# TensorE in source order, the other engines left to the build's scheduler: a two-layer FoX and NSA trunk

## The chip, the cores and the metric

The kernel runs on one core of one Trainium2 chip. A core has five engines that run at the same time, each with an instruction queue of its own: TensorE (PE; its weight loads are listed apart as PEld), VectorE (DVE), ScalarE (ACT), GpSimd (POOL) and SyncE (SP), which here issues nearly all DMAs. An engine works through its queue in order and waits at an instruction whose inputs have not been signalled. The metric is device time in microseconds (us) of one execution.

## The reference

The input is x, 512 tokens of 1024 channels. Each of two layers computes, all causal and in float32:

```
h    = rmsnorm(x);  proj = h @ w_in        # q,k,v,f | q_b, 6 x kv | gates
FoX:   8 heads of 64; s = q.k/8 + c_i - c_j, c = cumsum(log_sigmoid(f + b)); softmax; @ v
NSA:   8 query heads, 2 key heads, rope:
       compressed: blocks of 32 tokens -> gelu MLP -> one key/value a block; softmax over 31 blocks
       selected:   top min(16, 8) of 8 blocks of 64, so all causal keys
       window:     512 tokens, so all causal keys
       o = g0*o_c + g1*o_s + g2*o_w
mixed = sigmoid(ga) * (o_fox @ w_o_fox) + sigmoid(gb) * (o_nsa @ w_o_nsa)
x   += mixed @ w_out
x   += relu(rmsnorm(x) @ w_up)**2 @ w_down # 1024 -> 4096 -> 1024
```

A last rmsnorm follows the second layer. With 512 tokens the selection keeps every block and the window reaches every earlier token, so both branches are causal attention over 512 keys with their own keys and values.

## The kernel before

Activations lie transposed: channels on the 128 partitions, the 512 tokens along the free dimension. Nearly every product is split: a float32 operand becomes a rounded high part and a low part, and h·h, h·l and l·h are summed in PSUM. `gemm` (L212 to L214) does this for one output block of 128 channels: 8 blocks of the inner dimension times three products of 128x512, 24 in all; it is a generator that yields after every 6 products. Weights come by DMA in pieces of 128x1024 (`fetch`, L170), ACT rounds the high part (L186) and DVE subtracts the low part (L187) one piece ahead of its use.

PSUM has eight banks, handed out under four names with two buffers each: mm, S, PT, O. SBUF tiles are handed out by tag with a fixed number of buffers; the tag hl (a rounded key or query pair) has one, the tag e (scores of one head) two.

The source emits the work of a layer in this order.

1. `token_proj` multiplies for the FoX values (L315 to L317, 8 steps of 12 products of 128x512). `rstd` turns the sums of squares into the rmsnorm factor: column sums on PE (L267), a short chain on DVE and ACT (L270 to L278), and a broadcast on PE (L283). In layer 0 `rstd` is called after all 8 steps of the projection, in layer 1 after 6, with the other two emitted inside it, between L267 and L283. A second `token_proj` (128x288) gives the NSA values, forget logits and gates.
2. `forget` computes log_sigmoid of 32 columns in some 16 small DVE operations (L644 to L655), the running sum over tokens as products with a triangle (L662) and with ones (L661), and splits it into the tile CC (L663, L664).
3. `fox_proj(0)` projects the key pair and the query pair of the first two FoX heads. `k_pair` scales the projection (L336), rounds it into hl (L342, L343), copies it to the tile kd by four DMAs (L353) and adds two rows of CC (L357). `q_pair` does the same with four copies to q (L366) and two to qx (L375).
4. `attend` runs the eight FoX heads in rounds. Unit t (a head) gives its scores, four steps of two products (L392, L395), followed on DVE and ACT by mask and maximum (L398), exponential (L399) and, after the fourth, reciprocal and scaling (L403, L408). In the same rounds unit t-1 gives its transposes on PE (L421, three steps, read by L430 and L431), and unit t-2 its value products (L447, four steps). A unit takes five rounds. After each round the fill is advanced by 1.8 steps on average (`FOX_FILL`): further projections (`fox_proj(1)` to `(3)`, kc, vc, ks, two query pairs, kw), and, alternating with them, the steps of `compress`: block products with the compression weights (L525) and at its end, with no yield in between, transposes (L532), a gelu on DVE and ACT (L534 to L548), and two small products (L554, L558). Before a unit's first score the fill is advanced until the unit's projections have been emitted. What is left of the fill is emitted at the end.
5. A second `attend` runs 16 NSA units (a selected and a window branch for each head) with 0.95 fill steps a round (`NSA_FILL`). Its fill begins with `cmp_probs(0)`: scores against the compressed keys (L586), a copy (L589), transposes (L593), a softmax over blocks (L596 to L608) and transposes back (L612), all in one step. It goes on with gate projections (L838 scales them) and halves of the FoX output projection, the last two query pairs, `cmp_probs(1)` and eight more gate projections. A window branch ends with two products for the compressed values (L815).
6. The NSA output projection, the mix, and `wout`.
7. `mlp`: 8 plain blocks of `w_up` with `rstd` after the second, 12 blocks of the down projection, then 12 units in Strassen's form (L1196, seven products of 12 each) with the remaining down projections between the products, then the rest of `w_down`. The second layer ends in `last`, which does the final rmsnorm in two halves of 256 tokens.

This order is only the order of emission. `TileContext` records the instructions and their dependencies, and when the context closes the build's scheduler sets the order of every engine's queue: it plays the program through a model of the chip and gives each engine, among the instructions that are ready in the model, the one emitted earliest. So an engine's queue may have an instruction ahead of one that the source emits earlier. All of this happens in the build; on the chip the queues are fixed.

In the printed source, `go` starts with ten products on a tile of ones (L1087) before any data has arrived. The lines that the change touches stand in `build`:

Of the kernel before, what the change touches and what calls it, by code (L numbers as in the profile page):

```python
# [1284 lines left out]
def build(arrays):  # L1285
    nc = bacc.Bacc("TRN2", target_bir_lowering=False, num_devices=1)
    a = {k: nc.dram_tensor(k, v.shape, mybir.dt.from_np(v.dtype), kind="ExternalInput").ap()
         for k, v in arrays.items()}
    a["yT"] = nc.dram_tensor("yT", (2, 128, KT, T // 2), F32, kind="ExternalOutput").ap()
    with tile.TileContext(nc) as tc, ExitStack() as ctx:  # L1290
        Body(ctx, tc, nc, a).go()
    return nc


# [6 lines left out]
```

## Time and profile before

| what | value |
| --- | --- |
| median of 3 runs | 1554.0 us (1553.79 to 1554.16) |
| profiled execution | 1552.95 us |
| its span, first to last instruction | 1551.2 us |
| PE busy | 1536.4 us, 99% |
| PEld busy | 1306.6 us, 84% |
| DVE busy | 1075.2 us, 69% |
| ACT busy | 776.0 us, 50% |
| POOL busy | 205.2 us, 13% |
| mean granted TensorE clock | 0.998 |
| read from HBM | 140.77 MB |

The page gives the busy time of each engine and, in 40 slices, how busy each was. Its chain of waits goes back from the last instruction and is 95% PE. Matmuls are pipelined: a product of 128x512 is listed with some 0.39 us and the next begins some 0.23 us after it, so lengths overlap, and spacing is read from the start times. In the rows of the timeline the first number is the start, the second the length; out<-in are the program's names of tiles, and a bracket at the end gives the idle time of the engine before the row and what ended it. The rows of the view by stretches give the stretch, its length, the busy time of PE, PEld, DVE, ACT and POOL with the number of instructions, the granted clock, the DMA share and GB/s. The rows of the waits name who waited for whom, with total, number of times and longest.

### The profile page before, as it was taken

What the parts mean: (1) busy time and instruction counts of PE and PEld (TensorE: products, weight loads), DVE (VectorE), ACT (ScalarE), POOL (GpSimd) and SP (SyncE); (2) the same over time, 40 slices, a digit from 0 to 9 for tenths busy, and PEclk for the clock granted to TensorE, in tenths of its full rate; (3) what the DMA queues carried; (4) which work ended last, traced back from release to release, by engine and by line L of the source; (5) the groups of instructions that cost most, each with busy time, mean ns of one, the idle gap of its engine ahead of it and who ended that gap; (6) DMA issues with size and microseconds to landing.
All of it is one profiled execution on the core that took longest, in us unless ns stands there. A gap on an engine that the chain in (4) does not pass through costs nothing.

```text
span 1551.2 us, 22739 instructions
## 1 busy us (share of the span) xinstructions
PE 1536.4 (99%) x8460; PEld 1306.6 (84%) x8460; DVE 1075.2 (69%) x2204; ACT 776.0 (50%) x1455; POOL 205.2 (13%) x177
## 2 busy tenths in 40 slices
PE   9999999999999999999999999999999999999997
PEld 8877888888888999999887688888888889999997
DVE  5687988766569776664646789887664887766643
ACT  6444655553454555444433456555434635545553
POOL 4000000000201232221400000000002013222222
PEclk9999999999999999999999999999999999999999
DMA  7545422133333322321535543221433333323131
GB/s 240 172 128 154 127 82 82 55 114 117 96 95 123 109 96 95 109 82 64 176 117 165 157 140 100 68 82 55 150 95 95 95 120 99 113 91 99 65 96 55
DMA packets 56638, 169.57 MB, mean 109 GB/s; under 512 B 7344, under 2 KB 8112, under 8 KB 56528
## 3 DMA queue, kind: packets, MB, share of 16 engines
q1 hardware_dynamic: 53072, 161.84, 33.5%
q10 hardware_dynamic: 3456, 6.29, 1.2%
q8 instruction: 66, 1.08, 0.3%
q14 instruction: 44, 0.36, 0.1%
HBM read 140.77 MB, written 4.19 MB: 93 GB/s over the span
## 4 chain that ended last, share of the span: by engine, by line
PE 95%; DVE 3%; ACT 1%; issue 1%; POOL 0%; DMA 0%; DVEq 0%; SPq 0%; POOLq 0%; ACTq 0%
PE ps_mm L212 12%; PE ps_mm L213 12%; PE ps_mm L214 12%; PE ps_S L1196 4%; PE ps_O L1196 4%; PE ps_O L447 4%; PE ps_mm L1196 3%; PE ps_PT L421 3%; PE ps_PT L1196 3%; PE ps_S L212 3%; PE ps_S L213 3%; PE ps_S L214 3%; PE ps_PT L212 3%; PE ps_PT L213 3%; PE ps_PT L214 3%; PE ps_O L212 3%
## 5 line engine op out<-in xcount | busy, mean ns | idle before, releaser
L186 ACT CAST wh<-raw 128x1024 fp32r<-128x1024 f32 (+2 forms) x187 | 192.6, 1030 | 263.7 <-issue 58.5
L187 DVE TENSOR_TENSOR wl<-raw,wh 128x1024 fp32r<-128x1024 f32 (+2 forms) x187 | 226.6, 1212 | 49.8 <-ACT wh L186 48.9
L212 PE MATMUL ps_mm<-uh,wh 128*128 128x512 f32 x512 | 205.1, 401 | 0.0
L214 PE MATMUL ps_mm<-uh,wl 128*128 128x512 f32 x512 | 202.3, 395 | 0.0
L213 PE MATMUL ps_mm<-ul,wh 128*128 128x512 f32 x512 | 202.1, 395 | 0.0
L399 ACT ACTIVATE E<-E,mx 128x128 f32<-128x128 f32 x192 | 108.0, 563 | 82.7 <-DVE mx L398 75.6
L430 ACT CAST pth<-ps_PT 128x512 fp32r<-128x512 f32 x144 | 73.0, 512 | 94.7 <-PE ps_PT L421 94.4
L212 PEld LDWEIGHTS ps_mm<-uh,wh 128*128 128x128 f32 x512 | 96.2, 188 | 26.5 <-issue 10.6
L214 PEld LDWEIGHTS ps_mm<-uh,wl 128*128 128x128 f32 x512 | 96.2, 188 | 20.4 <-issue 0.8
L213 PE MATMUL ps_mm<-ol,wh 128*128 128x512 f32 (+1 forms) x288 | 111.5, 387 | 1.5 <-POOL ol L1263 1.5
L212 PE MATMUL ps_mm<-oh,wh 128*128 128x512 f32 (+1 forms) x288 | 111.8, 388 | 0.0
L214 PE MATMUL ps_mm<-oh,wl 128*128 128x512 f32 (+1 forms) x288 | 111.2, 386 | 0.0
L398 DVE CUSTOM_DVE_ANT_0 E<-ps_S,ct 128x128 f32<-128x128 f32 x192 | 92.2, 483 | 26.5 <-PE ps_S L395 25.0
L213 PEld LDWEIGHTS ps_mm<-ul,wh 128*128 128x128 f32 x512 | 96.4, 188 | 15.1
L431 DVE TENSOR_TENSOR ptl<-ps_PT,pth 128x512 fp32r<-128x512 f32 x144 | 85.0, 595 | 27.6 <-ACT pth L430 27.2
L1187 DVE TENSOR_TENSOR sl<-s,sh 128x512 fp32r<-128x512 f32 x96 | 76.6, 801 | 36.6 <-ACT sh L1186 36.3
L1263 POOL TENSOR_TENSOR ol<-c,oh 128x512 fp32r<-128x512 f32 x48 | 62.7, 1306 | 295.9 <-ACT oh L1262 268.3
L1186 ACT CAST sh<-raw 128x512 fp32r<-128x512 f32 x72 | 44.7, 620 | 106.3 <-PE ps_S L1196 48.1
L1186 ACT CAST sh<-s 128x512 fp32r<-128x512 f32 x96 | 59.3, 620 | 56.4 <-PE ps_PT L1196 19.3
L253 POOL TENSOR_TENSOR acc<-sq 128x512 f32<-128x512 f32 (+1 forms) x6 | 8.4, 1394 | 595.0 <-DVE wl L187 580.1
L421 PE MATMUL ps_PT<-ct,E 128*128 128x128 f32 x480 | 82.9, 273 | 1.4 <-DVE ptl L431 1.4
L421 PEld LDWEIGHTS ps_PT<-ct,E 128*128 128x128 f32 x480 | 60.1, 140 | 14.8 <-DVE ptl L431 4.2
(441 smaller groups left out, 4068.0 us busy)
## 6 DMA issues: line engine op xcount, KB each, us to landing
raw<-wb SPq DMA_DIRECT2D x64, 512.0 KB, 3.2
raw<-wup SPq DMA_DIRECT2D x64, 512.0 KB, 3.7
raw<-wd SPq DMA_DIRECT2D x48, 512.0 KB, 3.5
kd<-hl SPq DMA_DIRECT2D x48, 256.0 KB, 4.6
w<-w SPq DMA_DIRECT2D x32, 256.0 KB, 5.8
q<-hl SPq DMA_DIRECT2D x64, 128.0 KB, 3.2
raw<-wo SPq DMA_DIRECT2D x16, 512.0 KB
raw<-wout SPq DMA_DIRECT2D x16, 512.0 KB, 3.6
```

The source lines that it names most:

```text
L186: nc.scalar.copy(h[:, :n], raw[:, :n])
L187: nc.vector.tensor_tensor(lo[:, :n], raw[:, :n], h[:, :n].bitcast(F32), op=OP.subtract)
L212: mm(ps, h[:, c], xh, start=start and i == 0, stop=False)
L213: mm(ps, h[:, c], xl, start=False, stop=False)
L214: mm(ps, lo[:, c], xh, start=False, stop=stop and i == ks - 1)
L398: nc.vector.tensor_tensor_reduce(e, ps[:, :n], self.mask[:, T - n:], -1.0, BIG, OP.add, OP.min, mx)
L399: nc.scalar.activation(e, e, AF.Exp, bias=mx, scale=-1.0, accum_out=sm[:, i:i + 1])
L421: nc.tensor.transpose(ps[:, j * 128:(j + 1) * 128], E[i][:, b * 128:(b + 1) * 128], self.ident)
L431: nc.vector.tensor_sub(lo[:, o:o + n], ps[:, :n], h[:, o:o + n].bitcast(F32))
L1186: nc.scalar.copy(h, src)
L1187: nc.vector.tensor_tensor(lo, src, h.bitcast(F32), op=OP.subtract)
L1196: self.nc.tensor.matmul(ps, w, x, skip_group_check=True, **kw)
```

## The change

The body is traced inside a manual-schedule block for one engine. Instructions of TensorE that are emitted inside it keep the order of emission in TensorE's queue. The orders of DVE, ACT, POOL and SP are still chosen by the build's scheduler, which plays the same program with TensorE's order given. No instruction, shape, tile or buffer count is changed.

```diff
     with tile.TileContext(nc) as tc, ExitStack() as ctx:
-        Body(ctx, tc, nc, a).go()
+        with tc.manual_schedule(engines={mybir.EngineType.PE}):
+            Body(ctx, tc, nc, a).go()
     return nc
```

## The prediction

> **What bounds the kernel now.** I read the page's busy table and slices first, then what TensorE (PE) waits for, the stretches at both ends of the run, and then the timeline at each place where the source puts a dependent product right behind what it depends on.
>
> ```profile
> span 1551.2 us, 22739 instructions
> PE 1536.4 (99%) x8460; PEld 1306.6 (84%) x8460; DVE 1075.2 (69%) x2204; ACT 776.0 (50%) x1455; POOL 205.2 (13%) x177
> ...
> PE   9999999999999999999999999999999999999997
> ```
>
> PE is the bound, and it is busy in every slice: 14.8 us of the span are idle.
>
> ```profile
> 0.00:5.80 5.80, 4.64 (x20) 4.34 (x20) 1.40 (x4) 3.23 (x5) 4.82 (x13) 1.00 0.64 186
> 1536.00:1545.20 9.20, 6.59 (x54) 6.26 (x52) 1.95 (x8) 2.83 (x8) 1.48 (x2) 1.00 0.00 0
> 1545.20:1551.20 6.00, 0.00 (x0) 0.00 (x0) 2.43 (x8) 0.00 (x0) 0.00 (x0) 0.50 0.49 175
> ```
>
> The stretches by time (first figures: length, then PE busy) put 1.2 + 2.6 + 6.0 = 9.8 us of that idle time at the two ends. Only 5.0 us lie in the 1530 us between. Each chain of small vector work in there is covered by products that stand later in the source.
>
> ```profile
> PE ps_O L525 <- DVE ca L511: 1.4, 2, 0.7
> PE ps_O L283 <- DVE rcol L278: 1.4, 1, 1.4
> ```
>
> These two rows of the waits show what a waiting product does: PE stood 1.4 us at L283 in all, with the rest of that projection's products behind it. A product that waits holds what is queued after it. [...]
>
> **The change, part by part.** No instruction is added or removed; only PE's order changes. So the cost is the sum of chains that lose their cover, and the gain is at most the 5.0 us above. I take each chain from the trace, subtract vector work that stands in it only because products ran meanwhile, and subtract what the source itself emits in between. The two layers have the same code and the rows are of the first, so each term counts twice.
>
> *Forget gate.* The source calls `forget` (L662, L661) before the first key and query projections. PE runs 39 of those later products first:
>
> ```profile
> 42.64 0.30 PE L317 MATMUL ps_O<-wh,ul 128*128 128x288 f32 x1
> 42.77 0.39 PE L212 MATMUL ps_PT<-uh,wh 128*128 128x512 f32 x1
> 51.41 0.39 PE L214 MATMUL ps_PT<-uh,wl 128*128 128x512 f32 x1
> 51.88 0.38 PE L662 MATMUL ps_S<-ct,f 128*8 128x128 f32 x2
> ```
>
> ```profile
> 48.55 0.68 DVE L336 TENSOR_TENSOR tmp<-ps_PT,R 128x512 f32<-128x512 f32 x1
> 49.34 1.23 DVE L187 TENSOR_TENSOR wl<-raw,wh 128x1024 fp32r<-128x1024 f32 x1
> 50.59 0.68 DVE L343 SCALAR_TENSOR_TENSOR hl<-tmp,hl 128x512 fp32r<-128x512 f32 x1
> ```
>
> Spacing there is (51.41-42.77)/38 = 0.227 us a product. In source order PE stands from 42.77 until `forget`'s vector chain ends: 9.1 us as it runs now, less these three operations, which exist there only because of the advanced products (2.6): 6.5. Bounds: 5.3 (a second weight split of the same length drops out too) and 9.1.
>
> *First head pair.* `attend` emits its first score directly behind the query projection. The path is projection, scaling, the one `hl` buffer, copies to `kd`, then the same buffer for the query and copies to `q` and `qx`:
>
> ```profile
> 48.01 0.39 PE L214 MATMUL ps_PT<-uh,wl 128*128 128x512 f32 x1
> 51.30 3.97 SPq L353 DMA_DIRECT2D kd<-hl  x4
> 58.94 0.63 ACT L342 ACTIVATE hl<-tmp 128x512 fp32r<-128x512 f32 x1 [1.54 <-DMA kd<-hl]
> 59.68 2.62 SPq L366 DMA_DIRECT2D q<-hl  x4
> 62.34 1.24 SPq L375 DMA_DIRECT2D qx<-hl  x2
> 67.70 0.40 PE L395 MATMUL ps_S<-kd,qx 128*128 128x256 f32 x2
> ```
>
> The key's last product issues at 48.01, so its slot ends at 48.24; the first product that needs `qx` starts at 67.70, 19.5 us later. Only the query's 24 products (5.4) lie between in the source: 14.0, less the one split that now stands ahead of L343 (1.2): 13. Bounds 11.5 (some copies land sooner on an emptier queue) and 14. SP's queue issues the same copies in the same order, so nothing is saved there; the weight loads queued behind them only come later, and they lead by a block.
>
> *Fill of the first attention.* The fill alternates six products (6 x 0.227 = 1.36) with a step of the block compression:
>
> ```profile
> 95.14 0.65 PE L525 MATMUL ps_O<-w,ca 128*64 128x256 f32 x4
> 137.80 0.38 PE L532 MATMUL ps_S<-ct,tmp 128*128 128x128 f32 x2
> 143.44 0.66 PE L554 MATMUL ps_S<-G,small 128*128 128x64 f32 x4
> 141.82 1.23 DVE L187 TENSOR_TENSOR wl<-raw,wh 128x1024 fp32r<-128x1024 f32 x1 [0.24 <-DMA raw<-wb]
> ```
>
> Counted by the fill rate (1.8 steps a round, five rounds a head), the third pair's query is finished four steps before head 4 asks for it: 2 x 1.36 + 2 x 0.6 = 3.9, and about 1.2 of the heads' own products. The query's path is 0.7 + (67.70-58.94) = 9.5. Pause 4.4, taken as 4, with bounds 0 (SP and the buffer free early) and 9.5. The compression's end has no yield between L532 and L554: 143.44-138.07 = 5.4, less the split: 4 (bounds 3 and 5.4).
>
> *End of the first attention.* The fill is used up in head 7 (66 steps of the 90 that its rounds would take), so the transposes (L421) follow the last score (L395) with next to nothing between:
>
> ```profile
> 165.82 0.39 PE L395 MATMUL ps_S<-kd,qx 128*128 128x512 f32 x1
> 170.57 0.27 PE L421 MATMUL ps_PT<-ct,E 128*128 128x128 f32 x1
> ```
>
> 4.75 apart, of which 0.6 is products: 4 (bounds 2.5, 4.8).
>
> *Compressed probabilities.* `cmp_probs` emits scores, copy, transposes (L593), a softmax and transposes (L612) in one step, twice a layer:
>
> ```profile
> 252.59 0.60 PE L593 MATMUL ps_PT<-ct,tmp 128*128 128x128 f32 x4
> 259.60 0.63 PE L612 MATMUL ps_PT<-ct,tmp 128*128 128x128 f32 x4
> 253.84 0.68 DVE L838 TENSOR_TENSOR gate<-ps_mm,R 128x512 f32<-128x512 f32 x1
> 255.03 1.22 DVE L187 TENSOR_TENSOR wl<-raw,wh 128x1024 fp32r<-128x1024 f32 x1
> L589 ACT COPY tmp<-ps_S 128x512 f32<-128x512 f32 x1 | 0.6, 588 | 0.0
> ```
>
> 7.0 apart, 0.4 of it L593's own: 6.6; without the two foreign operations 4.7; with the copy ahead and its handovers (0.8) 5.5. One of the two may stay: 6 each, 12 a layer (bounds 11 and 15).
>
> *Head boundaries of the second attention.* 16 units; fill rate 0.95, so two rounds between the last score and the transposes hold 2 x 1.36 + 0.5 of products, and the fourth transpose is due 3.5 us after the score's start.
>
> ```profile
> 335.62 0.39 PE L395 MATMUL ps_S<-kd,q 128*128 128x512 f32 x1
> 338.35 1.28 DVE L408 TENSOR_SCALAR E<-E,rr 128x128 f32<-128x128 f32 x4
> 214.54 0.39 PE L395 MATMUL ps_S<-kd,q 128*128 128x512 f32 x1
> 219.91 1.27 DVE L408 TENSOR_SCALAR E<-E,rr 128x128 f32<-128x128 f32 x4
> ```
>
> L408 is the last step before them: it ends 4.0 after the score where the vector engine is calm, 6.6 where it is crowded (0.7 of that covered by L815 in every second unit). So a pause is 0.5 to 2.4. I take 0.9, nearer the calm end, since each pause lets the crowd drain: 14 a layer, bounds 8 and 38.
>
> *Normalizer and MLP.* In the MLP the trace already follows the source but for small pieces around the units' last product; taken at nothing, hidden by product 5's twelve products, a few tenths a unit if not. The exception is `rstd`:
>
> ```profile
> 439.70 0.95 PE L267 MATMUL ps_PT<-ones,acc 128*128 128x2 f32 x8
> 443.37 0.83 PE L283 MATMUL ps_O<-ct,rcol 128*128 128x128 f32 x6
> ```
>
> 2.9 filled by twelve products that the source emits afterwards; the chain alone about 2.2 (bounds 1.7, 2.9). It comes twice for the MLP and once more at the start of layer 0; layer 1's start has two steps emitted in between, and `last` splits its sums by hand.
>
> *Clock.*
>
> ```profile
> 1.06 4.64 PE L1087 MATMUL ps_PT<-ones 128*128 128x128 f32 x20 [1.06 <-DVE ones L1083]
> ```
>
> The opening products take 4.64/20 = 0.23 each, those of the same size at L283 about half, and the granted clock falls to 0.50 at 1545.20, 4.3 us after dense work ended at about 1540.9 (the row of the last stretch). The run now has no mid-run pause near that; the changed one would have four a layer (forget, head pair, two softmaxes). A restart with 4.64 us at half speed loses 2.3: bounds 0 and 18, taken as 12. [...]
>
> **The sum.** A layer: 6.5 + 13 + 4 + 4 + 4 + 12 + 14 + 2.2 = 59.7. Twice that, plus 2.2, plus 12 of clock: 133.6. The profiled execution took 1552.95 us (its span and 1.75 around it): 1687. The median shown, 1554.0, is 1.05 above it: **1688 us**, 8.6% slower. Low ends: 5.3 + 11.5 + 0 + 3 + 2.5 + 11 + 8 + 1.7 = 43 a layer, 1642 without clock. High ends: 9.1 + 14 + 9.5 + 5.4 + 4.8 + 15 + 38 + 2.9 = 98.7 a layer, 1772 with 18 of clock.
>
> **The rivals.**
> *Short chains (1642).* PE's pauses empty the vector and scalar queues, so each chain runs at its low end. For it: every chain measured has foreign operations in it. Against: the head pair is copies, which do not shorten.
> *Crowded rounds (1736).* All boundaries cost 2.4: 16 x 1.5 more a layer, 48 in all. For it: the fill's gates and splits sit in those rounds in the crowded row. Against: the calm row, and PE's load on the others falls as it pauses.
> *The other sign (1549).* The advanced products split transposes and value products apart, and undoing it returns the 5.0 us of idle time in mid-run. It decides only if fewer than 5 us of chains lose their cover in the whole run; the forget gate alone exceeds that unless its vector work is also done early, for which its input, the product at 42.64, leaves no room.
> *No effect (1554).* The order is already the source's. The 39 products ahead of L662 exclude it almost wholly.
>
> **How the numbers follow.** About 0.2% is what a measurement of this kernel can tell from no change. Forecast 0.61; crowded rounds 0.22; short chains 0.14; other sign 0.02; no effect 0.01. The range 1635 to 1755 leaves out a small part of the short case below its low ends and the crowded case with most other high ends, together under 2 in 10. Faster 0.02, same 0.01, slower 0.97.
>
> **What would show it.** After: PE idle of some 120 us or more in the busy table; L662 directly behind the L317 products with a DVE wait of 5 to 9 us; L395 waiting some 13 us for `qx`; L612 waiting for L608's result four times at 5 to 7 us; L554 and L283 with waits of 4 and 2; a granted clock below 1 in stretches behind the long pauses. Wrong would be: boundaries of several us each, buffers freed too late for PE's fixed order (a wait on a PSUM bank or on `hl` not named here), or the other engines' new order delaying weight splits so that plain projections wait.

## The result, and the profile after

The kernel with its products in source order takes 1724.8 us (median of four runs, 1722.5 to 1728.9), against 1553.9 before: a ratio of 1.110, with a 95% interval of 1.1077 to 1.1128. The forecast was 1688, in a range of 1635 to 1755. The profiled execution has a span of 1720.7 us against 1551.2, so 169.5 us are to be found.

The page of the changed kernel, span, busy table and slices:

```profile
span 1720.7 us, 22748 instructions
PE 1586.7 (92%) x8460; PEld 1342.0 (78%) x8460; DVE 1087.8 (63%) x2204; ACT 778.0 (45%) x1455; POOL 207.0 (12%) x177
...
PE   9698888699999999999987987978999999999998
...
PEclk9898899899999999999998988998999999999999
...
PE 84%; DVE 10%; ACT 2%; DMA 2%; issue 2%; SPq 1%; POOL 0%; DVEq 0%; ACTq 0%; POOLq 0%
```

TensorE has the same 8460 products (as the profile lists them: a product of unrounded float32 counts twice, so that the ten of L1087 stand there as x20). Its idle time went from 14.8 to 134.0 us (span less busy time), 119.2 more. Its busy time went from 1536.4 to 1586.7, 50.3 more for the same products. These two make up the 169.5. The slices show where: most holes lie in slices 2 to 8 and 21 to 28, the attention of the first and the second layer, and the granted clock has dents in the same places. The chain that ended last (the last line) now has 10% of vector work and 2% of copies in it.

What TensorE waited for (us in all, times, the longest):

```profile
PE ps_PT L421 <- DVE E L408: 24.2, 12, 5.5
PE ps_PT L612 <- DVE tmp L608: 19.8, 4, 5.0
PE ps_S L392 <- DMA q<-hl: 17.4, 2, 8.8
PE ps_S L586 <- DMA q<-hl: 17.1, 2, 8.8
PE ps_S L662 <- DVE f L655: 13.8, 2, 6.9
PE ps_S L554 <- DVE G L544: 8.9, 2, 4.4
PE ps_O L283 <- DVE rcol L278: 5.0, 3, 2.1
PE ps_S L395 <- DMA qx<-hl: 4.5, 4, 1.4
PE ps_PT L593 <- ACT tmp L589: 3.1, 4, 1.0
PE ps_S L1196 <- DVE c L1237: 2.6, 3, 1.5
PE ps_S L283 <- DVE rcol L278: 2.1, 1, 2.1
PE ps_O L1196 <- DVE c L1237: 1.1, 2, 0.6
```

Most rows are places that the prediction named. The fourth is not: L586 waiting for the copy of a query. No row names a weight split: the plain projections never starved.

How it looks in time, at the forget gate, at the second compressed scores and at the first compressed transposes of layer two (start, length, and in brackets the idle time before and who ended it):

```profile
45.19 0.29 PE L317 MATMUL ps_O<-wh,ul 128*128 128x288 f32 x1
52.37 0.60 PE L662 MATMUL ps_S<-ct,f 128*8 128x128 f32 x2 [6.88 <-DVE f L655]
...
298.19 1.10 PE L586 MATMUL ps_S<-q,kcz 128*128 128x512 f32 x4
308.12 2.05 PE L586 MATMUL ps_S<-q,kcz 128*128 128x512 f32 x4 [8.84 <-DMA q<-hl]
...
1070.17 1.08 PE L612 MATMUL ps_PT<-ct,tmp 128*128 128x128 f32 x4 [4.99 <-DVE tmp L608]
...
1071.69 0.63 PE L212 MATMUL ps_mm<-uh,wh 128*128 128x512 f32 x1
1072.12 0.63 PE L213 MATMUL ps_mm<-ul,wh 128*128 128x512 f32 x1
```

L662 now stands directly behind the L317 product, where 39 other products stood before. Those ran ahead of it there, so they need nothing from it, and now the first of them starts at 55.92, behind it: the waiting product held what was queued after it for 6.88 us. The prediction's row for this does not show it, since the 1.4 us at L283 lie at the run's end (1544.18), with only other products of L283 behind them. The last two rows show the second kind of loss: behind a pause, products start 0.43 us apart that start 0.227 us apart at full clock. The stretches of time around two pauses (length, PE busy with the number of products, granted clock, DMA share, GB/s):

```profile
299.30:304.19 4.89, 0.00 (x0) 1.00 0.59 171
304.19:321.25 17.06, 7.53 (x24) 0.50 0.15 44
321.25:324.67 3.42, 3.42 (x21) 1.00 0.00 0
519.23:522.64 3.41, 1.38 (x11) 1.00 0.06 24
522.64:526.06 3.42, 3.38 (x12) 0.50 0.54 158
526.06:529.47 3.41, 3.41 (x16) 1.00 0.00 0
```

The first three rows: the pause at L586 and the next one at L612 together hold the clock at 0.50 for 17.06 us, in which 24 products are made. The last three: behind a pause of only 2.1 us at the MLP's normalizer (L283), 3.42 us pass at half clock with hardly a gap in them. The profiled execution has 18 such stretches in mid-run, nine a layer, with a length of 3.41, 6.83, 10.24, 13.65 or 17.07 us. Where I set the distance between products inside them against the same products' usual distance in the kernel before, they lose some 38 to 41 us, by the way of counting. The other 9 to 12 of the 50.3 are at least in part a matter of listing: ahead of a pause, the 0.16 us by which a product's listed length (0.39) exceeds the spacing (0.23) count as busy, and the waits of PE are some 42 more than before, which gives 7 us as an estimate.

### The profile page after: what moved, and what is told of

It reads as the page before. It is cut to its first block, busy times and chain, and to the rows that moved or that the text cites. A ratio compares the mean times of both kernels' runs of the same rounds, so it can differ in the third digit from the quotient of the medians.

```text
span 1720.7 us, 22748 instructions
## 1 busy us (share of the span) xinstructions
PE 1586.7 (92%) x8460; PEld 1342.0 (78%) x8460; DVE 1087.8 (63%) x2204; ACT 778.0 (45%) x1455; POOL 207.0 (12%) x177
## 4 chain that ended last, share of the span: by engine, by line
PE 84%; DVE 10%; ACT 2%; DMA 2%; issue 2%; SPq 1%; POOL 0%; DVEq 0%; ACTq 0%; POOLq 0%
PE ps_mm L212 10%; PE ps_mm L213 10%; PE ps_mm L214 10%; PE ps_S L1196 4%; PE ps_O L1196 4%; PE ps_O L447 3%; PE ps_mm L1196 3%; PE ps_PT L1196 3%; PE ps_PT L421 3%; PE ps_PT L212 3%; PE ps_PT L213 3%; PE ps_PT L214 3%; PE ps_S L212 3%; PE ps_S L213 3%; PE ps_S L214 3%; PE ps_O L213 2%
## 5 line engine op out<-in xcount | busy, mean ns | idle before, releaser
L212 PE MATMUL ps_mm<-uh,wh 128*128 128x512 f32 x512 | 213.3, 417 | 0.0
L213 PE MATMUL ps_mm<-ul,wh 128*128 128x512 f32 x512 | 207.0, 404 | 0.0
L214 PE MATMUL ps_mm<-uh,wl 128*128 128x512 f32 x512 | 205.8, 402 | 0.0
L212 PEld LDWEIGHTS ps_mm<-uh,wh 128*128 128x128 f32 x512 | 100.8, 197 | 28.5 <-issue 11.3
L214 PEld LDWEIGHTS ps_mm<-uh,wl 128*128 128x128 f32 x512 | 100.1, 196 | 23.5
L213 PEld LDWEIGHTS ps_mm<-ul,wh 128*128 128x128 f32 x512 | 100.9, 197 | 16.1
L421 PE MATMUL ps_PT<-ct,E 128*128 128x128 f32 x480 | 87.3, 287 | 25.3 <-DVE E L408 24.2
L421 PEld LDWEIGHTS ps_PT<-ct,E 128*128 128x128 f32 x480 | 62.1, 146 | 37.4 <-issue 23.8
L1186 ACT CAST sh<-s 128x512 fp32r<-128x512 f32 x96 | 59.3, 620 | 57.1 <-PE ps_PT L1196 20.2
```

Source lines behind the costliest of these rows:

```text
L212: mm(ps, h[:, c], xh, start=start and i == 0, stop=False)
L213: mm(ps, h[:, c], xl, start=False, stop=False)
L214: mm(ps, lo[:, c], xh, start=False, stop=stop and i == ks - 1)
L421: nc.tensor.transpose(ps[:, j * 128:(j + 1) * 128], E[i][:, b * 128:(b + 1) * 128], self.ident)
L1186: nc.scalar.copy(h, src)
```

## The experiments

The theory: the loss is a sum of separate pauses, each at a place where the source has a dependent product right behind its cause, plus half clock behind them. The rivals: the loss is spread over all products (other engines' orders delaying splits or buffers); the pauses share one stock of covering work, so closing one opens another; the half clock is a small part.

**The order fixed in the MLP alone.** The attention is left to the scheduler.

```diff
-        return self.mlp(l, x, u, acc, gm)
+        with self.tc.manual_schedule(engines={mybir.EngineType.PE}):
+            return self.mlp(l, x, u, acc, gm)
```

> Only the MLP's products are held to the source's order; everything ahead of it is left to the scheduler. Theory (exposed chains, then half clock): the MLP has one chain of 2.2 us a layer behind the column sums, two or three pauses of 0.7 to 1.6 us in the Strassen units and one stretch of 3.4 us at half clock, so some 2.2 + 3 + 1.5 a layer: 1560 to 1568 us. Rival (the fixed order itself makes products or the other engines' queues slower everywhere): the MLP is about half of TensorE's time, so half of the added 171 us, some 1640.

Measured: 1564.0 us (1562.3 to 1564.2), ratio 1.0064 (1.0049 to 1.0079). Some 10 of the 171 us belong to the MLP, so the loss is not spread over all products. The time lies within what was expected. Its waits are the normalizer (1.4 us of the first row stood at L283 before the change too) and the pieces between the MLP's units:

```profile
PE ps_O L283 <- DVE rcol L278: 3.4, 2, 2.1
PE ps_S L1197 <- DVE c L1238: 2.5, 3, 1.4
PE ps_S L283 <- DVE rcol L278: 2.1, 1, 2.1
```

**The pauses kept, the clock kept up.** The changed kernel with throwaway products of ones in its long pauses. They go to a bank whose content is overwritten, so the result is the same.

```diff
+    def keep(self, ps, n):
+        for _ in range(n):
+            self.nc.tensor.matmul(ps[:, :128], self.ones, self.ones, start=True, stop=True)
...
+        self.keep(pt, 22)
...
+        self.keep(ps, 30)
...
+        self.keep(self.p("S"), 38)
```

The three calls shown stand ahead of L612, of L662 and of the first attention. In the same way 20 products stand ahead of L554, 24 ahead of head 7's transposes, 38 inside the second L586 group and 8 ahead of the MLP's normalizer.

> The changed kernel with throwaway products of ones (128x128, 0.22 us each) placed where TensorE stands longest: 30 ahead of the forget sums, 38 ahead of the first score, 20 ahead of the compression's last products, 24 ahead of head 7's transposes, 22 ahead of each of the two transposes behind a softmax, 38 inside the second compressed scores, 8 ahead of the MLP's broadcast. They are shorter than the pauses and write banks that are overwritten, so every chain ends when it did, and the result is the same. Theory (about 38 us of the added time are products at half clock behind pauses): 30 us less, some 1695 us, and granted clock 1 almost everywhere. Rival (half clock falls into time that is lost anyway, the whole 171 us are pauses): within 6 us of 1725. Rival (throwaway work delays the real one): above 1731.

Measured: 1696.8 us (1692.6 to 1702.0), ratio 1.092 (1.0899 to 1.0945). The page:

```profile
span 1690.8 us, 24366 instructions
PE 1644.2 (97%) x9268; PEld 1407.4 (83%) x9268; DVE 1087.4 (64%) x2204; ACT 778.7 (46%) x1455; POOL 207.3 (12%) x177
```

404 throwaway products, listed as 808, and 28 us less time. The half clock is therefore worth at least 28 of the 171 us. The two profiled executions show the rest. The throwaway products take 93.0 of the 1644.2 us, so the kernel's own take 1551.2, which is 35.5 less than in the changed kernel; idle time and throwaway products together are 139.6 us, which is 5.6 more than the changed kernel's idle time, probably because some outlast their pause. The difference of the two, 29.9 us, is that of the spans. The mean granted clock went from 0.957 to 0.994, and four stretches of 3.41 us remain, in which about 6 us are lost by the distances. With the 35.5 that makes some 41, as read above.

**The compressed probabilities cut into steps.** `cmp_probs` yields behind its copy and four times ahead of its transposes, and alternates with a gated block.

```diff
@@ cmp_probs, behind the copy (L589)
+        yield
@@ ahead of the transposes back (L612)
+        for _ in range(4):
+            yield
@@ fill2
-            yield from cmp_gen(0)
-            yield from gated(0)
+            yield from alternate(cmp_gen(0), gated(0))
...
-            yield from cmp_gen(1)
-            yield from gated(4)
+            yield from alternate(cmp_gen(1), gated(4))
```

> The changed kernel with one part of the source's order undone: the compressed softmax gives way between its parts to steps of the gate projections (one step of six products between scores and transposes, four between transposes and transposes back). Theory: the four pauses of 5.2 us and four of 0.9 go (24 us) and with them part of the half-clock stretches behind them (2 to 3 us each in layer halves without another pause near): 1690 to 1700 us. Rival (the vector engine's softmax only moves the wait to the next head boundary): less than 12 us gained.

Measured: 1703.8 us (1703.2 to 1708.4), ratio 1.097 (1.0956 to 1.0989): 21 us gained. The two rows of L612 and L593 (22.9 us) are gone from the waits, but one row grew:

```profile
PE ps_PT L421 <- DVE E L408: 32.4, 20, 5.5
```

From 24.2 us in 12 waits to 32.4 in 20: 8 us came back at the head boundaries, and the time lies 4 us above what was expected. The reading is that the vector engine cleared the boundaries' work while TensorE stood at L612, and is late there without the stop. The run with throwaway products bears it out: its pauses last at least as long, with a faster clock behind them, and its L421 row has 13.2 us in 10 waits, the same as the changed kernel without the two waits of 5.5 us that were filled.

**The fourth query projected earlier**, a gated block ahead of its place, so that a block of products lies between it and the second compressed scores.

```diff
@@ fill2
             yield from qproj(2)
+            yield from qproj(3)
             yield from gated(2)
-            yield from qproj(3)
             yield from cmp_gen(1)
@@ the order of the weight loads
-            if m in (1, 3):
-                yield wb[14 + m // 2], 1024
+            if m == 1:
+                yield from ((wb[i], 1024) for i in (14, 15))
```

> The changed kernel with the last query pair's projection emitted right behind the third's, ahead of two gate projections, instead of directly ahead of the compressed scores that read it. Theory: the pause of 9.0 us a layer inside the second compressed scores, a copy of the query by DMA, has 60 products as cover and goes; the half-clock stretch of 17 us there shrinks: 18 to 22 us less, 1703 to 1707 us. Rival (the copy waits for the query buffer, of which there are three for four pairs, and not for its projection): nothing gained, or the wait moves to the next pair.

Measured: 1711.5 us (1709.2 to 1712.7), ratio 1.101 (1.0992 to 1.1029): 13 us gained, where 18 to 22 were expected. The L586 row (17.1) is gone; again part returns at the boundaries:

```profile
PE ps_PT L421 <- DVE E L408: 27.7, 14, 5.5
```

The clock's part of the gain did not come: TensorE is idle for 13.2 us less than in the changed kernel, but its busy time is 1590.1 us, 3.4 more, with 20 half-clock stretches in mid-run in place of 18.

**The forget gate's sums behind the first key and query products.**

```diff
@@ ahead of the call of forget
+        early = []
+        for i in range(2):
+            w = self.weights(wb[i])
+            early.append(self.p("PT"))
+            run(self.gemm(early[-1], w, 0, u))
@@ behind it
-        run(fox_proj(0, ("PT", "PT")))
+        st["ka", 0] = self.k_pair(self.scaled(early[0]), 0)
+        st["qa", 0] = self.q_pair(self.scaled(early[1]), True)
```

> The changed kernel, but the source emits the products of the first key block and the first query block ahead of the forget gate's sums, as the scheduler of the kernel before did; their scaling stays behind the sums. Theory: the pause at L662 (7.04 and about 6.8 us, 13.8 in the waits view) is a dependent product standing directly behind its cause; with 48 products of 0.227 us (10.9 us) between, it goes. The half-clock stretch of 6.83 us behind it goes too, worth about 1 to 2 us a layer. The head pair's wait is nearly unchanged, since the query's chain still begins after the same products. Expected some 16 us less than the changed kernel, 1707 to 1711. Rival: the key's and query's scaling now waits for the sums, so the copies of the first head start later and the wait at L392 grows by what L662 gives up: 1720 to 1725, with L392 at some 15 us a layer.

Measured: 1698.5 us (1697.6 to 1703.2), ratio 1.094 (1.0923 to 1.0956): 26 us gained where 16 was expected, so the rival falls and the theory was too low. Two rows of the timeline show one reason:

```profile
60.05 0.38 PE L662 MATMUL ps_S<-ct,f 128*8 128x128 f32 x2
67.20 0.55 PE L392 MATMUL ps_S<-kd,q 128*128 128x256 f32 x1 [6.77 <-DMA q<-hl]
```

The sums themselves now run inside the head pair's wait, which falls from 17.4 to 13.5 us for both layers. With the 13.8 of L662 that is 17.7, of which L586, waiting 1.1 longer, takes some back: TensorE is idle for 16.5 us less. Its busy time is 1580.1 us, 6.6 less, as the loss inside the half-clock stretches fell by 5 to 6 us. That makes 23.1, the distance between the two profiled executions; the medians lie 26 apart. The pause filled with products that had to be made anyway paid twice here, 16.5 us in idle time and 6.6 in busy time.

**Eight fill steps ahead of the first score.**

```diff
-        self.attend([fox_unit(h) for h in range(8)], fill1(), self.FOX_FILL)
+        fill = fill1()
+        for _ in range(8):
+            next(fill)
+        self.attend([fox_unit(h) for h in range(8)], fill, self.FOX_FILL)
```

> The changed kernel, but eight steps of the first attention's fill (some 48 products of the next blocks, 10.9 us, and four compression steps) are emitted ahead of its first score. Theory: the first score stands 8.8 us in each layer, and about 1.8 more at the next one, because nothing stands between the query's projection and the score; the eight steps cover it, and its half-clock stretch of 10.24 us goes: 8.8 + 1.8 + up to 4 of clock a layer. The fill is the same amount of work, so it is used up eight steps earlier, and the last head boundaries have none: up to two more boundaries of 4 to 5 us each a layer. Net 10 to 28 us less, 1697 to 1715. Rival: the pause is only moved to the end of the attention, since the sum of the chains that lack cover is the same: 1720 to 1728.

Measured: 1711.5 us (1710.3 to 1712.9), ratio 1.1015 (1.0997 to 1.1033): 13 us gained out of the 20 that the head pair had cost. The 17.4 of L392 is gone from the waits, but there is a new wait, on a load whose lateness cost 1 us in all until then:

```profile
142.62 1.72 PE L525 MATMUL ps_O<-w,ca 128*64 128x256 f32 x4 [5.98 <-DMA w<-w]
```

The queue of SP shows where the load is issued:

```profile
133.59 3.81 SPq L353 DMA_DIRECT2D kd<-hl  x4
139.24 0.53 SPq L357 DMA_DIRECT2D kd<-CC  x1
139.82 0.86 SPq L520 DMA_DIRECT2D w<-w  x2
```

The compression's weights (L520) are issued behind the copies of the next head pair. The compression was brought forward on TensorE, the place of its loads among the copies was not. This wait comes once a layer, 11.8 us in all. That earlier loads would close it was not tried.

**All four edits together** (the three edits of the source's order above and the eight fill steps).

> All four edits of the source's order at once: forget gate's sums behind the first key and query products, the compressed probabilities cut into three steps that alternate with a gated block, the fourth query block ahead of the second compressed scores' predecessor block, eight fill steps ahead of the first score. Each names one place at which the product order of the source has a dependent product behind its cause. Theory: the pauses are separate terms, so the gains add: about 21 + 13 + 16 + 10 to 25 less than the changed kernel's 1725, that is 1650 to 1665, and what is left is head boundaries (some 35 us), smaller pauses and the clock behind them. Rival: the fill is one stock of products, so what covers one pause is missing at another; then the gains overlap and the time is 1675 to 1695.

Measured: 1655.6 us (1653.9 to 1656.2), ratio 1.0655 (1.0639 to 1.0671). Alone the edits gained 21.0 + 13.3 + 26.3 + 13.3 = 73.9 us, together 69.3. They add within 5 us, and the time lies below the 1675 to 1695 of the rival of one shared stock, which falls: the gains are nearly separate terms. What is left:

```profile
PE ps_PT L421 <- DVE E L408: 37.7, 26, 4.1
PE ps_O L525 <- DMA w<-w: 11.6, 2, 5.9
PE ps_S L554 <- DVE G L544: 5.9, 2, 2.9
PE ps_O L283 <- DVE rcol L278: 5.0, 3, 2.1
```

Four pauses are gone, and 13.5 us of them have come back as many small ones at L421. The kernel before remains the fastest. That a second buffer for `hl` or a cut through the compression's end (L554) would return more was not tried.

**Pauses of graded length.** To see what drops the clock, pauses were put into places that have none: a chain of two-column operations that hangs on a block's result, and a product of two columns that waits for it. The chain's length varies from place to place.

```diff
+    def pause(self, src, n):
+        nc = self.nc
+        z = self.t("s4", [128, 2], name="pz")
+        nc.vector.tensor_scalar(z, src[:, :2], 1.0, None, op0=OP.mult)
+        for _ in range(n):
+            nc.vector.tensor_scalar(z, z, 1.0, None, op0=OP.mult)
+        nc.tensor.matmul(self.bank()[:, :2], self.ones, z, start=True, stop=True)
...
+            if m % 2:
+                self.pause(x[m], 2 * m - 2 + 2 * l)
```

> The changed kernel with 22 pauses put in at places that have none: after an output block, a plain block or a block of the MLP's second half, a chain of n+1 two-column vector operations (n from 0 to 14 in steps of two) hangs on the block's result, and a product of two columns waits for it. The result is the same. Each chain should hold TensorE for 1 us and some 0.2 us for each further operation, so 1 to 4.5 us. Theory A: the clock falls behind a pause only when the pause exceeds a fixed length, somewhere between 2 and 4 us; short rungs leave the clock at 1 and long ones all lead to half-clock stretches. Theory B: it falls by windows of fixed phase (the stretches seen so far are multiples of 3.41 us), so that rungs of 2 to 3.4 us sometimes lead to a stretch and sometimes not, and those above 3.4 always do. Time 1725 plus the pauses (40 to 70) plus 1.7 for each stretch (15 to 30).

Measured: 1856.3 us (one execution). The rungs missed their lengths: the links queued among other vector work, so that all but a few came out at 4.2 to 7.9 us instead of 1 to 4.5, and all of these led to half clock. It tells the theories apart poorly. What it gave was the grid: each half-clock stretch in it, as in the changed kernel, begins a multiple of 3.413 us behind the first one. The second ladder has shorter rungs.

```diff
-            nc.vector.tensor_scalar(z, z, 1.0, None, op0=OP.mult)
+            nc.gpsimd.tensor_scalar(z, z, 1.0, None, op0=OP.mult)
...
-                self.pause(x[m], 2 * m - 2 + 2 * l)
+                self.pause(x[m], m // 2 + 4 * l)
```

> The ladder again with shorter rungs: its chains stood among other vector work and came out at 4.2 to 7.9 us, nearly all of which led to half clock. Here the links behind the first stand on the engine that is idle there, from 0 to 7 of them a pause, 22 pauses. The result is the same. Expected pauses from 1 to some 4 us and a time of 1725 plus 30 to 70. Theory: the clock is set anew at fixed instants 3.413 us apart (every half-clock stretch of the changed kernel begins on that grid), from the idle time between the two instants before: a pause of less than half of that (1.7 us) never leads to a stretch, one of more than 3.4 always, and one between does where most of it lies within one interval. Rival: each pause above one fixed length leads to a stretch that begins a fixed time behind its start, on no grid.

Measured: 1832.7 us (one execution); slower than expected, since the idle engine's links too were longer than estimated (a median of 0.52 us each). Its rungs run from 1.1 to 7.7 us. Two of them decide. The pauses in the timeline:

```profile
494.45 0.38 PE L262 MATMUL ps_S<-pz,ones 128*128 128x2 f32 x2 [2.29 <-POOL pz L261]
...
510.40 0.38 PE L262 MATMUL ps_mm<-pz,ones 128*128 128x2 f32 x2 [2.94 <-POOL pz L261]
```

And the stretches between the instants of the grid around them:

```profile
491.93:495.34 3.41, 1.12 (x7) 1.00 0.06 6
495.34:498.75 3.41, 3.41 (x10) 0.50 0.48 148
505.58:508.99 3.41, 1.87 (x9) 1.00 0.36 131
508.99:512.41 3.42, 2.01 (x10) 1.00 0.53 141
512.41:515.82 3.41, 3.41 (x17) 1.00 0.03 12
```

The shorter pause, 2.29 us, lies wholly in one interval: PE is busy for 1.12 of 3.41 us, and the next interval is at 0.50. The longer one, 2.94, lies across an instant: the two intervals keep 1.87 and 2.01 us of work, and the clock stays at 1.00. A fixed length of pause can't give this order, so the rival falls. Two other pauses, of 2.24 us, led to half clock as well. Counted over the ten traces with the products' order fixed (the changed kernel and nine experiments), for intervals at full clock:

```
idle time in the interval    intervals    next one at half clock
under 1.4 us                 4374           1
1.4 to 2.0 us                 114          45
over 2.0 us                   126         126
```

In these traces the border lies between 1.4 and 2.0 us, around half of the interval. It is as sharp as the listed lengths of products, whose ends the profiler models; each kernel gave one trace.

## Why the prediction was right, and where it was wrong

The direction held, and the rival "short chains" (1642), the other sign and "no effect" are out. So is "crowded rounds" (1736), although its time is near the measured one: its mechanism did not happen. The forecast was 37 us low, and by the profiles nearly all of that is one term.

By the prediction's steps, both layers, predicted against the waits above:

| step | predicted, us | measured, us |
|---|---|---|
| forget gate (L662) | 13 | 13.8 |
| first head pair (L392 for `q`, two of the L395 for `qx`) | 26 | 20.2 |
| query of head 4 (the other two of the L395) | 8 | about 2 |
| compression's end (L554) | 8 | 8.9 |
| end of the first attention (L421, two at 5.5) | 8 | 11.0 |
| compressed probabilities (L612, L593) | 24 | 22.9 |
| head boundaries of the second attention (rest of L421) | 28 | 13.2 |
| normalizer (L283, without the 1.4 in `last` that stood there before) | 6.6 | 5.8 |
| MLP's units (L1196) | 0 | 3.7 |
| second compressed scores (L586) | not named | 17.1 |
| all pauses | 121.6 | 119.2 (idle time of the page, less that of before) |
| clock | 12 | 50.3 more busy time; at least 28 by experiment, 38 to 41 by the distances |

*The failed step is "Clock".* It took four restarts a layer behind the long pauses, each with the 4.64 us of the opening products. There were nine a layer, one of them behind a pause of 2.1 us (L283) and one behind one of 2.8 (L421), and where pauses follow each other within 12 us (L586 and L612) the clock did not come back in between, for 17 us. The price of one was about right (2.1 to 2.3 us a stretch, where 2.3 was the most assumed); the count and the chained ones were not. The upper bound of 18 was set by the same count and so missed too.

*The sum of the pauses was right by cancelling.* Missed was the query copy ahead of the second compressed scores: the fill emits `qproj(3)` directly ahead of `cmp_gen(1)`, whose later score products need it. This is the same pattern as the first head pair, which I had costed; the fill's order was read for its blocks and not for which head the compressed scores read. The experiment with the early query confirms it: the wait goes, 13 us return. Too high were the boundaries: 32 times 0.9 were assumed, and only 8 of them waited visibly (the 12 waits of the L421 row less the two at the end of the first attention; at two boundaries TensorE waited twice). The argument that each pause lets the vector engine catch up was right and went further than taken; the experiments show it from the other side, since closing a pause at L586, at L612 or all four made L421 wait more (24.2 us to 27.7, 32.4 and 37.7); closing that at L662 did not change it. Too low was the end of the first attention, at 5.5 us a layer above its bound of 4.8.

Too high, too, were the head pair and head 4, and the traces show the step. The prediction took 67.70, where the first product that needs `qx` stood before, for the end of the copies. But that row has no wait: products of another block stand ahead of it, and the copies may have been ready earlier. In the changed kernel the same product does wait:

```profile
75.28 1.24 SPq L375 DMA_DIRECT2D qx<-hl  x2
77.69 0.55 PE L395 MATMUL ps_S<-kd,qx 128*128 128x256 f32 x1 [1.33 <-DMA qx<-hl]
```

From the start of that issue to the product are 2.41 us here, and 67.70 - 62.34 = 5.36 in the prediction's rows. The 2.95 us between are no part of the chain. Without them the head pair's 14.0 become 11.1; in the changed kernel the key's products end at 61.54, so the same distance is 77.69 - 61.54 - 5.4 = 10.7, of which TensorE is idle for 10.0. The split of 1.2 that the prediction subtracted stands ahead of L343 there too. Head 4's pause of 4.4 becomes 1.5, near its measured 1. Both steps used the same difference, which is about 12 us in all over the two layers.

*Where the mechanism was named, it held.* L662, L612, L554 and L283 wait for the producers that were predicted, at 6.9, 5.0, 4.4 and 2.1 us at the longest. The head pair stands at the copy to `q` first (L392, 8.8) and at `qx` for only 1.4, where the prediction had the whole wait at `qx`. The fear that other engines would delay the splits did not come true; a likely reason is the 119 us more of standing products in which they can run ahead.

## What to carry to other kernels

Fixed by the source, this kernel's order of products needed other products emitted between each result and its first use, as many as the whole chain takes, copies and buffer handovers included (the first head pair lacked 10.7 us of them). Without them such a place was a pause, of up to 8.8 us in one wait, and these pauses added: the four edits gained 73.9 us one by one and 69.3 together. Price such a pause twice: its own length, and the half clock that follows it, which took some 38 to 41 us over 18 stretches here. In these traces half clock followed each time TensorE was idle for over 2.0 us of one 3.41 us interval (126 of 126), and in 45 of 114 cases between 1.4 and 2.0; the pause of 2.1 us at L283 was already enough. When a pause is closed by bringing work forward, look at the place of that work's loads on their queue too (L525 then waited 5.98 us for its load). And read the length of a chain from a row that waits for it: a row without a wait gives only an upper bound (5.36 us at `qx`, where the row that waits gave 2.41).

## What the runs showed of the hardware that was not expected

The granted clock fell and rose in mid-run only at instants 3.413 us apart, and no pause moved them: in each of the ten traces all half-clock stretches begin on one grid, and those in mid-run last a whole number of intervals (41 intervals in 18 stretches of the changed kernel). What went with the clock of an interval was the idle time within the one before: over 2.0 us of 3.41 half clock followed in 126 of 126, under 1.4 in 1 of 4374, in between in 45 of 114. Counted from the first instruction, the grid does not lie at the same place in every trace (its first instant comes at 0.40 us in the changed kernel's and at 0.08 in the first ladder's), and the same pause cost an interval in one and nothing in another: the 1.6 us at the first normalizer (L283 in layer 0) led to half clock in seven of the nine traces in which the order is fixed there, and not in the changed kernel's, where it lies across an instant. This may be why four executions of the changed kernel spread over 6.4 us, the slowest with the lowest mean clock (0.951 against 0.957), while those before the change spread over 0.5; no run tests it. Whether the border is a share of busy time or a count of work done in the interval is not told apart by these runs.
